# Block 1 works on rows that are not yet normed: the norm applied when results leave PSUM, and the modulation sums tied to their place

## The chip, the cores and the metric

The kernel is one program on one core of a Trainium2 chip. The metric is the device time of one execution in microseconds (us): the median of several runs, lower is better.

## What is computed

Two blocks follow each other on 256 tokens of width 1024, all in float32. Block 1 has two layers, and the change lies in them:

```python
def hybrid_layer(x, gain, w_in, f_bias, w_branch, w_out):
    h = rms_norm(x, gain)                       # x * rsqrt(mean(x*x) + eps) * gain
    proj = jnp.einsum('bsd,de->bse', h, w_in)
    (qa, ka, va, ga, qb, kb_, vb_, gb, qc, kc, vc, gc,
     q_idx, k_idx, w_idx, f_logit, merge_logit) = jnp.split(proj, SPLIT_POINTS, axis=-1)
    ...
    # branch a: attention with rotary positions; branch b: the same over the keys that an
    # index (q_idx, k_idx, w_idx) selects; branch c: attention with forgetting (f_logit)
    y = jnp.einsum('nbsw,nwd->bsnd', jnp.stack([oa, ob, oc], axis=0), w_branch)
    merged = jnp.sum(jax.nn.sigmoid(merge_logit).reshape(B, S, N_BRANCH, D_MODEL) * y, axis=2)
    return x + jnp.einsum('bsd,de->bse', merged, w_out)
```

The second block (a Fourier and gating mixer, a neighbourhood attention, two gated feed-forward nets) is modulated by six vectors of each layer, `silu(c) @ ada_w + ada_b`, for two conditions.

The norm's factor is one number per token. So `rms_norm(x, gain) @ W` equals `(x * gain) @ W` with each token's row scaled afterwards.

## The kernel before, in words

Every product of activations and weights is done three times, with both split in a rounded high part and a remainder (`hh`, `hl` for activations, `whi`, `wlo` for weights): high by high, high by low, low by high. TensorE (PE) takes 128 tokens or 128 features at a time.

Weights come in pieces of 512 KB (`piece`, L159 to L173): SP issues the load into one of three `raw` buffers, ScalarE (ACT) writes `whi` (L171), VectorE (DVE) writes `wlo` (L172), and with that the raw buffer is free for the next load. A chunk is four pieces, 1024 by 512 weights. SP is one queue, and a load that waits for its buffer holds back what is behind it.

**The head of layer 0 (L813 to L844).** PE is kept busy by ten products on a tile of zeros (`keep_up`, L252 to L254). For each of the two rows of 128 tokens: ACT squares two halves of x and adds them up (L294), a root and a few DVE steps make the factor (`rstd`, L305 to L320), DVE scales the row (`xs`, L325), PE turns it in eight transposes of 128x128 (L341), ACT and DVE evacuate them with the gain (`hf`, L351 and L347), ACT writes `hh` (L356), DVE writes `hl` (L358). The weight splits are held behind the norm on their engines (`behind`). Then `layer(0, ...)` begins.

**A layer (L444 to L811)** runs: the first chunk (index queries, `heads_T` with kind "first": row 0's 24 products, then row 1's), the small projections (`psm`: index keys, index weights, forget logits), the four chunks of branch a (q, k, v, gate), the selection for branch b, branch b's chunks between the parts of branch a's attention, branch c's, three merges, and `w_out` in two column halves, whose second half gives row 0, then row 1. As soon as a row is finished, `done0` squares, norms, turns and splits it for layer 1.

**The modulation sums (`ada`, L372 to L426)** are done on DVE: for each 512 KB tile of `ada_w` and each condition one multiply-add over 1024 columns (L417 the first of a group, L419 the rest); after eight tiles PE adds up the partitions (`reduce`, L384 to L396, product L388 `pada`), and the result goes to memory. A generator yields one tile at a time; `fill` (L179) advances it two steps at every second call, from the end of branch a's attention on. That is the place in the program. The tool that lays out the queues orders each engine's instructions by when it thinks that they can start, and among those by place in the program, so these sums may be issued much earlier than they are written.

The index scores of the selection go through `psc`'s two PSUM buffers too (tag "at"); ACT evacuates them (`r`, L662), and DVE weighs them (L667).

Of the kernel before, what the change touches and what calls it, by code (L numbers as in the profile page):

```python
# [92 lines left out]
def tile_model(ctx: ExitStack, tc: tile.TileContext, A: dict, out: bass.AP, dbg=None):  # L93
# [170 lines left out]

    def mm_feat(ps, pieces, m, xh, xl):
        mm_group(pieces, [feat_target(ps, m, xh, xl)])
# [14 lines left out]
    class Row:  # L281
# [51 lines left out]
        def norm_steps(self, gains, shifts, hh, hl, o, last, xs=None, even=False):  # L333
            if xs is None:
                xs = self.scaled()
            for g in range(2):
# [35 lines left out]
    def ada(tasks):  # L372
# [28 lines left out]
        for i, (layer, g, k) in enumerate(tiles):  # L401
# [24 lines left out]
    def block1(pa):  # L426
# [17 lines left out]
        def layer(l, hT, done, first):  # L444
            W = A["w_in"][l]
            hh, hl = hT

            def tok(t):
                return slice(t * P, (t + 1) * P)

            def heads_T(pieces, kind, scale, dst):

                pss = [ps_mm(nm("pq")) for t in range(2)]
                tg = [tok_target(pss[t], hh, hl, tok(t)) for t in range(2)]
# [25 lines left out]
            def values(pieces):  # L480
                v = pt.tile([P, 2, 512], F32, tag="v", bufs=2, name=nm("v"))
                pss = [ps_mm(nm("pv")) for t in range(2)]
                mm_group(pieces, [tok_target(pss[t], hh, hl, tok(t)) for t in range(2)])
                for t in range(2):
                    ACT.activation(v[:, t, :], pss[t], AF.Copy)
# [93 lines left out]
            mm_feat(ps[:, :S], sw, 0, hh, hl)  # L579
# [6 lines left out]
            DVE.tensor_copy(sm, ps[:, :S])  # L586
# [96 lines left out]
            def project(b):  # L683
# [5 lines left out]
                def heads(i, scale, dst):  # L689
                    if b < 2:  # L690
                        heads_T(chunk(W[4 * b + i]), "rope", scale, dst)
# [3 lines left out]
                def v_():  # L695
                    r["v"] = values(chunk(W[4 * b + 2]))
# [91 lines left out]
            for c2 in range(2):  # L788
# [30 lines left out]
        w0 = pa.tile([P, 1], F32, name="w0")  # L819
        ACT.activation(w0, one, AF.Sqrt)  # L820
# [649 lines left out]
```

## Time and profile before

| | us |
|---|---|
| median of 3 runs | 1599.95 |
| lowest, highest | 1597.28, 1603.94 |
| the profiled execution | 1600.51 |
| its span, first to last instruction | 1598.7 |
| PE busy | 1574.8 (99%) |
| VectorE (DVE) busy | 1187.3 (74%) |
| ScalarE (ACT) busy | 796.4 (50%) |

An engine's busy time is the union of its instructions. PE's instructions are recorded with a modelled end: products of 512 columns are shown with 0.40 us each while they start every 0.23 us, so PE's throughput is read from starts. PEclk is the clock that PE was granted, as a share of 2.4 GHz; 0.5 is 1.2 GHz.

### The profile page before, as it was taken

To read this page: it belongs to the slowest core of one execution; us is meant where nothing else is said; L and a number is where in the kernel's file an instruction comes from. 1 tells how busy PE (TensorE), PEld (TensorE's weight loads), DVE (VectorE), ACT (ScalarE), POOL (GpSimd) and SP (SyncE) were. 2 spreads that over 40 slices of the span, in tenths; PEclk is the share of its full clock that TensorE was granted. 3 is DMA by queue.
4 is the path that set the end of the run, shared out by engine and by line. 5 is a ranking of instruction groups with operands and counts; after the bars stand their busy time and mean duration, and the time that the engine had idled before them with its cause. 6 is when DMAs were issued, how large, how long until landed. Compare 5 with 4: busy or idle time off the path is not lost.

```text
span 1598.7 us, 24860 instructions
## 1 busy us (share of the span) xinstructions
PE 1574.8 (99%) x9397; PEld 1325.4 (83%) x9397; DVE 1187.3 (74%) x2262; ACT 796.4 (50%) x1351; POOL 29.0 (2%) x45
## 2 busy tenths in 40 slices
PE   9999999999999999999999999999999999999999
PEld 7868898978888999878898877877787677679897
DVE  7996557877877779888678599776668656588773
ACT  6555545555555455664354332333345545576551
POOL 0000000000000000000000000000000201000000
PEclk9999999999999999999999999999999999999999
DMA  7753555746445757544335356755535323367650
GB/s 259 243 174 120 158 184 171 226 143 202 150 142 190 222 175 236 171 169 136 96 117 183 106 196 221 248 190 176 180 104 147 97 68 113 91 220 242 210 181 27
DMA packets 81496, 267.21 MB, mean 167 GB/s; under 512 B 10400, under 2 KB 16736, under 8 KB 81376
## 3 DMA queue, kind: packets, MB, share of 16 engines
q1 hardware_dynamic: 81376, 265.62, 52.3%
q8 instruction: 74, 1.21, 0.3%
q14 instruction: 46, 0.38, 0.1%
HBM read 264.45 MB, written 1.13 MB: 166 GB/s over the span
## 4 chain that ended last, share of the span: by engine, by line
PE 86%; DVE 6%; ACT 3%; DMA 3%; issue 2%; SPq 0%; DVEq 0%; ACTq 0%
PE pfg L239 4%; PE pfg L241 4%; PE pfd L1201 4%; PE pfv L241 4%; PE pfv L239 4%; PE pfv L240 4%; PE pfg L240 4%; PE pfd L1203 4%; PE pfd L1202 4%; PE pmg L239 3%; PE pmg L241 3%; PE pmg L240 2%; DVE wlo L172 2%; PE pq L231 2%; PE psc L515 2%
## 5 line engine op out<-in xcount | busy, mean ns | idle before, releaser
L171 ACT ACTIVATE whi<-raw 128x1024 fp32r<-128x1024 f32 x390 | 407.3, 1050 | 396.7 <-PE pfd L1203 51.7
L172 DVE TENSOR_TENSOR wlo<-raw,whi 128x1024 fp32r<-128x1024 f32 x390 | 470.0, 1211 | 156.8 <-ACT whi L171 154.7
L419 DVE SCALAR_TENSOR_TENSOR adaa<-adaw,cs,adaa 128x1024 f32<-128x1024 f32 x140 | 176.8, 1279 | 11.9 <-DMA adaw<-in_ada_w 11.4
L241 PE MATMUL pfg<-hh,wlo 128*128 128x256 f32 (+1 forms) x352 | 117.7, 334 | 0.0
L239 PE MATMUL pfg<-hh,whi 128*128 128x256 f32 (+1 forms) x352 | 117.5, 334 | 0.1
L239 PE MATMUL pfv<-hh,whi 128*128 128x256 f32 (+1 forms) x352 | 117.3, 333 | 0.1
L241 PE MATMUL pfv<-hh,wlo 128*128 128x256 f32 (+1 forms) x352 | 117.3, 333 | 0.0
L240 PE MATMUL pfv<-hl,whi 128*128 128x256 f32 (+1 forms) x352 | 116.9, 332 | 0.0
L240 PE MATMUL pfg<-hl,whi 128*128 128x256 f32 (+1 forms) x352 | 116.7, 331 | 0.0
L239 PE MATMUL pmg<-hh,whi 128*128 128x256 f32 x384 | 108.2, 282 | 0.0
L241 PE MATMUL pmg<-hh,wlo 128*128 128x256 f32 x384 | 107.7, 280 | 0.0
L240 PE MATMUL pmg<-hl,whi 128*128 128x256 f32 x384 | 107.3, 279 | 0.0
L1201 PE MATMUL pfd<-whi,gh 128*128 128x512 f32 (+1 forms) x275 | 105.7, 386 | 0.0
L1203 PE MATMUL pfd<-whi,gl 128*128 128x512 f32 (+1 forms) x275 | 105.7, 384 | 0.0
L1202 PE MATMUL pfd<-wlo,gh 128*128 128x512 f32 (+1 forms) x275 | 105.5, 384 | 0.0
L239 PEld LDWEIGHTS pfg<-hh,whi 128*128 128x128 f32 x352 | 66.2, 188 | 8.5 <-issue 1.5
L239 PEld LDWEIGHTS pmg<-hh,whi 128*128 128x128 f32 x384 | 72.2, 188 | 1.2 <-issue 0.8
L240 PEld LDWEIGHTS pfv<-hl,whi 128*128 128x128 f32 x352 | 66.3, 188 | 7.5
L240 PEld LDWEIGHTS pfg<-hl,whi 128*128 128x128 f32 x352 | 66.3, 188 | 7.5
L239 PEld LDWEIGHTS pfv<-hh,whi 128*128 128x128 f32 x352 | 66.1, 188 | 7.5 <-issue 0.5
L240 PEld LDWEIGHTS pmg<-hl,whi 128*128 128x128 f32 x384 | 72.2, 188 | 0.2 <-issue 0.2
L241 PEld LDWEIGHTS pmg<-hh,wlo 128*128 128x128 f32 x384 | 72.2, 188 | 0.0
(338 smaller groups left out, 3801.6 us busy)
## 6 DMA issues: line engine op xcount, KB each, us to landing
raw<-in_w_in SPq DMA_DIRECT2D x152, 512.0 KB
adaw<-in_ada_w SPq DMA_DIRECT2D x96, 512.0 KB
raw<-in_ffn_up SPq DMA_DIRECT2D x96, 512.0 KB
raw<-in_ffn_down SPq DMA_DIRECT2D x40, 512.0 KB
raw<-in_w_branch SPq DMA_DIRECT2D x24, 512.0 KB
raw<-in_odd_qkv SPq DMA_DIRECT2D x24, 512.0 KB
raw<-in_w_out SPq DMA_DIRECT2D x16, 512.0 KB
raw<-in_even_in SPq DMA_DIRECT2D x12, 512.0 KB
```

The costliest lines, as they stand in the source:

```text
L171: behind(ACT.activation(hi, raw, AF.Copy))
L172: behind(DVE.tensor_sub(lo, raw, hi.bitcast(F32)))
L231: PE.matmul(ps, xl[:, k, tsl], hi, start=False, stop=last)
L239: PE.matmul(ps, hi[:, msl], xh[:, k, :], start=first, stop=False)
L240: PE.matmul(ps, hi[:, msl], xl[:, k, :], start=False, stop=False)
L241: PE.matmul(ps, lo[:, msl], xh[:, k, :], start=False, stop=last)
L419: behind(DVE.scalar_tensor_tensor(acc[:, s, :], raw, c, acc[:, s, :], op0=ALU.mult, op1=ALU.add))
L515: PE.matmul(pss[j][:, o_:o_ + n], qT[64 * j:64 * j + 64, hp, qs_], kT[64 * j:64 * j + 64, hp, ks_], start=terms is None, stop=True)
L1201: PE.matmul(ps, gh[:, k, tsl], hi[:, i, csl], start=k == 0, stop=False)
L1202: PE.matmul(ps, gh[:, k, tsl], lo[:, i, csl], start=False, stop=False)
L1203: PE.matmul(ps, gl[:, k, tsl], hi[:, i, csl], start=False, stop=k == NH - 1)
```

## The change

In both layers, the first chunk, the small projections and branch a's q, k and v are computed from `x * gain` (tiles `raw`), without the norm's factor. The factor is worked out meanwhile (`roots`) and multiplied in where ACT or DVE takes the result out of PSUM. After branch a's k, `normalize` makes the normed `hh` and `hl` for all later chunks: two small products spread the factors of the tokens over the partitions, and DVE and ACT scale and split the turned rows again. In layer 0 the three products of a piece run as high by high, low by high, high by low, row 0 then row 1, piece by piece (`mm_parts`). At the boundary of the layers the rows are turned column half by column half as the halves of `w_out` finish, each of them queued for the end of a group of products (`later`). In the head, the identity is loaded ahead of x, row 1 of x after the first piece of weights, and ten filler products become four and eight (the eight on x). The modulation sums are pinned: none is issued ahead of the DVE instruction that is written just before it. The activations with a root, at the head and at the boundary, go away in block 1's layer 0.

```diff
+    SP.dma_start(cst[:, 0:P], A["cst"][:, 0:P])
     for n in range(2):
         SP.dma_start(x_sb[:, 0, n * 512:n * 512 + 512], A["x"][0:P, n * 512:n * 512 + 512])
-    SP.dma_start(cst[:, 0:P], A["cst"][:, 0:P])
     SP.dma_start(vec, A["vec"])
-    SP.dma_start(x_sb[:, 1, :], A["x"][P:2 * P, :])
...
+    def pinned(ins):
+        behind(ins)
+        tc.keep_in_program_order(ins)
...
+    def mm_parts(rows_, pieces, xh, xl):
+        n, k0 = len(pieces), 0
+        for j, (hi, lo, nk) in enumerate(pieces):
+            for ps, tsl in rows_:
+                for part, (x_, w_) in enumerate(((xh, hi), (xl, hi), (xh, lo))):
+                    for i in range(nk):
+                        p_ = PE.matmul(ps, x_[:, k0 + i, tsl], w_[:, i, :], start=j == part == i == 0,
+                                       stop=j == n - 1 and part == 2 and i == nk - 1)
+                        if part == i == 0:
+                            tc.keep_in_program_order(p_)
+            k0 += nk
...
-                    behind(DVE.tensor_scalar_mul(acc[:, s, :], raw, c))
+                    pinned(DVE.tensor_scalar_mul(acc[:, s, :], raw, c))
...
-                    behind(DVE.scalar_tensor_tensor(acc[:, s, :], raw, c, acc[:, s, :], op0=ALU.mult, op1=ALU.add))
+                    pinned(DVE.scalar_tensor_tensor(acc[:, s, :], raw, c, acc[:, s, :], op0=ALU.mult, op1=ALU.add))
...
+            def normalize():
+                ps = ps_tr(nm("prb"))
+                for t in range(2):
+                    b_ = sp.tile([P, P], F32, tag="t512", bufs=4, name=nm("rb"))
+                    DVE.tensor_scalar_mul(b_, C("ones"), rs[0][:, t:t + 1])
+                    PE.matmul(ps[:, tok(t)], b_, ident, start=True, stop=True)
+                rb = pt.tile([P, S], F32, tag="t256", bufs=3, name=nm("rb"))
+                DVE.tensor_copy(rb, ps[:, :S])
+                for g in range(2):
+                    ks = slice(4 * g, 4 * g + 4)
+                    f = sp.tile([P, 4, S], F32, tag="big", bufs=2, name=nm("hn"))
+                    tc.keep_in_program_order(DVE.tensor_add(f, rh[:, ks, :].bitcast(F32), rl[:, ks, :].bitcast(F32)))
+                    DVE.tensor_mul(f, f, rb.unsqueeze(1).broadcast_to([P, 4, S]))
+                    split_to(hh[:, ks, :], hl[:, ks, :], f)
...
                 if kind == "first":
-                    for t in range(2):
-                        mm_group(pieces, [tg[t]])
-                else:
-                    mm_group(pieces, tg)
+                    rs.append(root())
+                    rs.append(sp.tile([P, 2], F32, tag="rs8", bufs=1, name=nm("rs8")))
+                    DVE.tensor_scalar_mul(rs[1], rs[0], 0.125)
...
-                    ACT.activation(qs, ps, AF.Copy, scale=scale)
+                    ACT.activation(qs, ps, AF.Copy, scale=scale if kind == "rope" else r_[:, t:t + 1])
...
+                if f is steps[1]:
+                    normalize()
...
-                        xr[t].square(a, w)
+                        if l == 1:
+                            xr[t].square(a, w)
...
                     load_ahead(*first)
+                    if l == 0:
+                        later(turn_first)
...
+        def roots():
+            ss = sp.tile([P, 2, 2], F32, tag="rss", bufs=8, name=nm("rss"))
+            for t in range(2):
+                for n in range(2):
+                    junk = sp.tile([P, 512], BF16, tag="jx", bufs=1, name=nm("junk"))
+                    behind(ACT.activation(junk, x_sb[:, t, n * 512:n * 512 + 512], AF.Square, accum_out=ss[:, t, n:n + 1]))
+            v = sp.tile([P, 2], F32, tag="rsv", bufs=8, name=nm("rsv"))
+            DVE.tensor_add(v, ss[:, :, 0], ss[:, :, 1])
+            DVE.tensor_scalar(v, v, 1.0 / D, EPS, op0=ALU.mult, op1=ALU.add)
+            return rsqrt(v, 2)
+
+        def turn_first():
+            raw_tiles()
+            for t in range(2):
+                turn(t, 0)
...
         with tc.high_priority():
-            keep_up(ps, 10, idle)
+            keep_up(ps, 4, idle)
+        turn(0, 0, True)
+        load_ahead("qi0", A["w_in"][0][12], 1)
+        SP.dma_start(x_sb[:, 1, :], A["x"][P:2 * P, :])
+        keep_up(ps, 8, x_sb[:, 0, :])
+        turn(0, 1)
+        turn(1, 0, True)
+        load_ahead("qi0", A["w_in"][0][12], 2)
+        turn(1, 1, True)
         load_ahead("qi0", A["w_in"][0][12])
...
         def done0(t):
-            if t == 0:
-                nxt.append(h_tiles())
-            xr[t].norm_T(V("ng1"), None, nxt[0][0], nxt[0][1], t * P, True)
-            if t == 0:
-                load_ahead("qi1", A["w_in"][1][12])
+            def rest():
+                turn(t, 1, True)
+                if t == 0:
+                    load_ahead("qi1", A["w_in"][1][12])
+            later(rest)
```

`turn(t, g)` transposes four 128-column blocks of row t (half g of the columns) and writes `raw`'s high and low part with the gain, by the steps that `norm_steps` had. `rsqrt` (L269 to L280) is eleven small DVE steps.

## Rows read from the trace of the kernel before

**Rows 1.** The page's first part: busy us (share of the span) xinstructions.

```profile
PE 1574.8 (99%) x9397; PEld 1325.4 (83%) x9397; DVE 1187.3 (74%) x2262; ACT 796.4 (50%) x1351; POOL 29.0 (2%) x45
```

**Rows 2.** Table of stretches: length, busy PE, PEld, DVE, ACT, POOL; PEclk, DMA, GB/s.

```profile
26.00:60.00 34.00, 33.12 (x181) 26.60 (x180) 30.88 (x68) 18.32 (x24) 0.00 (x0) 1.00 0.80 263
...
82.00:98.00 16.00, 12.96 (x46) 9.45 (x45) 13.75 (x40) 7.82 (x17) 0.00 (x0) 0.79 0.46 143
...
110.00:240.00 130.00, 129.71 (x975) 115.99 (x973) 79.98 (x170) 69.89 (x127) 0.00 (x0) 1.00 0.51 159
340.00:362.00 22.00, 20.23 (x93) 15.51 (x92) 17.69 (x31) 13.69 (x28) 1.25 (x4) 0.92 0.37 120
362.00:440.00 78.00, 77.43 (x431) 63.73 (x430) 63.33 (x180) 44.68 (x68) 0.00 (x0) 1.00 0.56 172
```

**Rows 3.** The same table over the first part of each of the two layers.

```profile
20.00:110.00 90.00, 86.07 (x459) 69.82 (x458) 81.03 (x197) 50.32 (x78) 0.00 (x0) 0.96 0.68 219
340.00:440.00 100.00, 97.66 (x521) 79.24 (x520) 81.02 (x210) 58.37 (x95) 1.25 (x4) 0.98 0.52 161
```

**Rows 4.** The table of stretches, for the tile `adaa` alone: PE, PEld and DVE.

```profile
20.00:110.00 90.00, 0.00 (x0) 0.00 (x0) 19.29 (x16) 0.96 0.68 219
```

**Rows 5.** Timeline of the head, PE: start, us, instruction [idle before <-releaser].

```profile
1.48 6.87 PE L254 MATMUL pidle<-idle 128*128 128x256 f32 x20 [1.48 <-DVE idle L823]
...
8.63 1.89 PE L254 MATMUL pidle<-xs 128*128 128x256 f32 x8
...
11.40 0.49 PE L229 MATMUL pq<-whi,hh 128*128 128x512 f32 x1 [0.44 <-ACT hh L356]
...
25.29 0.40 PE L230 MATMUL pq<-wlo,hh 128*128 128x512 f32 x1
25.52 0.39 PE L231 MATMUL pq<-whi,hl 128*128 128x512 f32 x1
```

**Rows 6.** Timeline of the head, ACT and DVE.

```profile
3.51 0.63 ACT L294 ACTIVATE junk<-x_sb 128x512 bf16<-128x512 f32 x1 [1.28 <-DMA x_sb<-in_x]
...
8.93 0.86 ACT L351 ACTIVATE hf<-pT,vec 128x128 f32<-128x128 f32 x3
...
9.82 0.35 DVE L347 TENSOR_SCALAR hf<-pT,vec 128x128 f32<-128x128 f32 x1 [0.42 <-ACT hf L351]
...
10.73 0.61 ACT L356 ACTIVATE hh<-hf 128x512 fp32r<-128x512 f32 x1
```

**Rows 7.** Timeline of PE, then of ACT, where layer 0's branch a begins to attend.

```profile
88.12 2.13 PE L515 MATMUL psc<-qk 64*128 64x128 f32 x8 [2.48 <-ACT r L662]
...
86.53 1.06 ACT L171 ACTIVATE whi<-raw 128x1024 fp32r<-128x1024 f32 x1 [2.49 <-DMA raw<-in_w_in]
87.49 1.07 ACT L662 ACTIVATE r<-pix 128x512 f32<-128x512 f32 x2
```

**Rows 8.** What SP's queue waited for, 0 to 110 us: total, times, longest.

```profile
SPq L168 <- DVE wlo L172: 38.1, 14, 8.0
```

**Rows 9.** Timeline of PE at the boundary of the layers.

```profile
352.09 0.66 PE L469 MATMUL pqT<-cst,qs 128*128 128x128 f32 x4 [1.12 <-DVE hf L347]
...
354.13 0.66 PE L231 MATMUL pq<-whi,hl 128*128 128x512 f32 x1 [0.55 <-DVE hl L358]
```

**Rows 10.** Groups by line, 0 to 60 us: count | busy us, mean ns | idle before.

```profile
L606 PE MATMUL pcum<-lf,cst 128*128 128x8 f32 x2 | 0.4, 256 | 0.0
...
L172 DVE TENSOR_TENSOR wlo<-raw,whi 128x1024 fp32r<-128x1024 f32 x18 | 21.8, 1222 | 3.8 <-ACT whi L171 3.7
...
L586 DVE COPY sm<-psm 128x256 f32<-128x256 f32 x1 | 0.4, 418 | 0.0
...
L319 DVE SCALAR_TENSOR_TENSOR rsy<-rst,rsy 128x1 f32<-128x1 f32 x2 | 0.3, 159 | 0.1
```

**Rows 11.** The tile `adaa` over the span: durations min/median/max ns; idle time ahead (us, times).

```profile
L419 DVE SCALAR_TENSOR_TENSOR adaa<-adaw,cs,adaa x140: 1252/1280/1292, 31.2 to 1167.5; 128x1024 f32<-128x1024 f32 x140
...
  DMA adaw<-in_ada_w: 11.4, 10
```

More of the change, by code (lines that the diff above doesn't have):

```diff
@@ L331, in norm_T, with norm_steps @@
                 pass
-        def norm_steps(self, gains, shifts, hh, hl, o, last, xs=None, even=False):
+        def norm_steps(self, gains, shifts, hh, hl, o, last, xs=None, even=False, halves=(0, 1)):
             if xs is None:
                 xs = self.scaled()
-            for g in range(2):
+            for g in halves:
                 ps = ps_tr(nm("pT"))
@@ L442, in rope, with layer @@
             DVE.tensor_add(q3[:, :, 0:16], q3[:, :, 0:16], tmp)
-        def layer(l, hT, done, first):
+        def layer(l, raw, hT, root, done, first):
             W = A["w_in"][l]
             hh, hl = hT
+            rh, rl = raw
+            rs = []
             def tok(t):
                 return slice(t * P, (t + 1) * P)
+            def normalize():
[12 more added lines that the diff above has]
+                    split_to(hh[:, ks, :], hl[:, ks, :], f)
@@ L451, in heads_T @@
             def heads_T(pieces, kind, scale, dst):
                 pss = [ps_mm(nm("pq")) for t in range(2)]
-                tg = [tok_target(pss[t], hh, hl, tok(t)) for t in range(2)]
-                if kind == "first":
-                    for t in range(2):
-                        mm_group(pieces, [tg[t]])
-                else:
-                    mm_group(pieces, tg)
+                xh, xl = (hh, hl) if kind == "rope" else raw
+                if kind == "first" and l == 0:
+                    mm_parts([(pss[t], tok(t)) for t in range(2)], pieces, xh, xl)
+                elif kind == "first":
+                    for t in range(2):
+                        mm_group(pieces, [tok_target(pss[t], xh, xl, tok(t))])
+                else:
+                    mm_group(pieces, [tok_target(pss[t], xh, xl, tok(t)) for t in range(2)])
@@ L478, in plain_T, with values @@
                 fill()
-            def values(pieces):
+            def values(pieces, b):
                 v = pt.tile([P, 2, 512], F32, tag="v", bufs=2, name=nm("v"))
                 pss = [ps_mm(nm("pv")) for t in range(2)]
-                mm_group(pieces, [tok_target(pss[t], hh, hl, tok(t)) for t in range(2)])
+                mm_group(pieces, [tok_target(pss[t], *((hh, hl) if b else raw), tok(t)) for t in range(2)])
                 for t in range(2):
-                    ACT.activation(v[:, t, :], pss[t], AF.Copy)
+                    ACT.activation(v[:, t, :], pss[t], AF.Copy, scale=1.0 if b else rs[0][:, t:t + 1])
                 fill()
@@ L690, in heads @@
                     if b < 2:
-                        heads_T(chunk(W[4 * b + i]), "rope", scale, dst)
+                        heads_T(chunk(W[4 * b + i]), "rope" if b else "raw", scale, dst)
                     else:
@@ L818, in block1, with raw_tiles, turn @@
         hT = h_tiles()
-        w0 = pa.tile([P, 1], F32, name="w0")
-        ACT.activation(w0, one, AF.Sqrt)
+        raw = []
+        def raw_tiles():
+            raw[:] = [pa.tile([P, KD, S], F32R, tag=g, bufs=n, name=nm("raw" + g)) for g, n in (("mac", 1), ("qk", 3))]
+        raw_tiles()
+        def turn(t, g, last=False):
+            for _ in xr[t].norm_steps(V(turn.gain), None, *raw, t * P, last, xr[t].ap, halves=(g,)):
+                pass
+        def roots():
+            ss = sp.tile([P, 2, 2], F32, tag="rss", bufs=8, name=nm("rss"))
+            for t in range(2):
+                for n in range(2):
[6 more added lines that the diff above has]
+        def turn_first():
+            raw_tiles()
+            for t in range(2):
+                turn(t, 0)
+        turn.gain = "ng0"
         idle = sp.tile([P, 512], F32, tag="t512", bufs=4, name="idle")
@@ L825, in block1 @@
         with tc.high_priority():
-            keep_up(ps, 10, idle)
+            keep_up(ps, 4, idle)
[7 more added lines that the diff above has]
+        turn(1, 1, True)
         load_ahead("qi0", A["w_in"][0][12])
         SP.dma_start(cst[:, P:], A["cst"][:, P:_C1])
-        with tc.high_priority():
-            for t in range(2):
-                for n in range(2):
-                    xr[t].square(n * 512)
-                xs = xr[t].scaled()
-                steps = xr[t].norm_steps(V("ng0"), None, hT[0], hT[1], t * P, t == 1, xs)
-                if t == 0:
-                    for _ in range(5):
-                        next(steps)
-                    keep_up(ps, 4, xs)
-                for _ in steps:
-                    pass
         for l in range(2):
@@ L862, in done1 @@
                 xr[t].square(n * 512)
-        layer(0, hT, done0, ("qi1", A["w_in"][1][12], 2))
+        turn.gain = "ng1"
+        layer(0, raw, hT, roots, done0, ("qi1", A["w_in"][1][12], 2))
         filler[0] = None
@@ L867, in block1 @@
         SP.dma_start(fg, A["final_gain"][0:1, :].broadcast_to([P, D]))
-        layer(1, nxt[0], done1, ("ev", A["even_in"][2], 2))
+        layer(1, raw, hT, roots, done1, ("ev", A["even_in"][2], 2))
     xr = [Row(x_sb[:, t, :]) for t in range(2)]
```

10 lines of the change are left out of this document (5 added, 5 removed).

## The prediction

> **What bounds the kernel now.** I read the page first: PE is busy for 99% of the span, DVE for 74% [rows 1]. So the time can only fall where PE idles, runs at its lower clock or does work that the result doesn't need, and such places have to be looked for one by one. The table of stretches shows three in block 1's layer 0 and at the boundary to layer 1. In 82 to 98 us PE is busy 12.96 of 16.00 us, 3.04 short, and its mean granted clock is 0.79; since the clock has two levels, 2.4 and 1.2 GHz, 0.21 of 16 us, 3.36 us, is lost on top: 6.40 us. In 340 to 362 us it is 1.77 us of idling and 0.08 x 22 = 1.76 us of clock: 3.53 us. In 26 to 60 us it is 0.88 us [rows 2]. Elsewhere in these parts it is little: 0.57 us in 362 to 440, 0.29 us in 110 to 240 [rows 2]. The fourth place is the head: the first real product starts at 11.40 us, the last of the first chunk at 25.52 us [rows 5].
>
> Then the timeline, for the causes. In the head the first 14 us go into reading x, squares, the factor, the scaled row, transposes and splits, one behind the other [rows 6]. At 85 to 88 us PE waits 2.48 us for ACT's `r`; ACT itself had sat 2.49 us for a piece of weights, with `r` queued behind that split [rows 7]. The piece was late because SP waits for raw buffers: 38.1 us in 14 waits for DVE's `wlo` up to 110 us [rows 8]. So the engine behind the stall is DVE: busy 81.03 of 90 us there, of which 19.29 us are modulation sums, issued long before their place in the program [rows 3, 4]. At the boundary PE waits for the turned row 1, 1.12 and 0.55 us, and then runs at 1.2 GHz for a while [rows 2, 9].
>
> **The change, part by part.** Sums are made against the profiled execution, 1600.51 us (span 1598.7 and 1.8 around it); it lies 0.56 us above the median of the runs shown.
>
> *Head.* The squares, the factor and the scaled row go from the path; the transposes wait for x alone, whose first half is there at 3.51 us, and for PE, which first does eight filler instructions instead of twenty. Twenty took 6.87 us from 1.48 on, so eight end at about 1.48 + 8/20 x 6.87 = 4.2 us. The first four transposes end near 4.8. Then stand sixteen filler instructions on x (each product is recorded as two), at 1.89/8 = 0.24 us [rows 5]: to 8.6 us. The other transposes, and with them the first product, which is pinned behind the last of them, wait for that and for PSUM: its two transpose buffers are freed by ACT's 0.86 and DVE's 0.35 us [rows 6], so the last four run near 10.5 to 11 us. The first product starts at about 11.4 us, as now. What is won is the stretch behind it: 48 products at 25.52 - 25.29 = 0.23 us are 11.2 us, and they took 25.52 + 0.23 - 11.40 = 14.35 us because row 1's norm was in between [rows 5]. ACT has four times 0.86 + 0.61 for the rows [rows 6] and four splits of 1.06 [rows 7], 10.1 us between 4.8 and 18: they keep up. I take 0.5 us for waits: end at 23.1, **2.7 us won**. The bounds: with the filler fitted into waits the first product starts at 8.6, the end is 11.2 and some 1.5 us of transposes later, 21.3: 4.4 won. At the other end, PE at its lower clock at the start: in 82 to 98 us a drop cost 3.36 us [rows 2], which would leave 0.7 us lost. I take full clock, because x is there at 3.51 us, before the filler ends, so that PE has work without a break from 1.48 us on. The Trainium skill (TensorE: Matmul & The Clock Gate, What's actually happening) says that PE's default state is the throttled one and that activity releases it, which speaks against cutting the filler; by it the head would be at the lower bound if PE paused between filler and transposes, and no row of before shows such a pause.
>
> The squares (four of 0.63 on ACT [rows 6]) and the factor (some 14 DVE steps of 0.16 [rows 10], 2.2 us) now lie beside PE's first chunk and small projections; if that cover is gone, the evacuation of the first chunk comes up to 2 us late. SP's queue is moved too: row 1 of x goes behind the first piece of weights, which is so ahead of it by 512 KB; no cost, since row 1 is wanted after the filler.
>
> *Pinned sums.* The first sum can't be issued before branch c's second chunk, past 110 us. So 19.29 us leave DVE's 81.03 [rows 3, 4], and SP's loads of `ada_w` no longer stand in between. Layer 1 is the comparison: the same code in 362 to 440 us, with hardly any sums and DVE at 63.33 of 78, loses 0.57 us [rows 2]. I take **5.8 of the 6.40 us** in 82 to 98, and **0.4 of the 0.88** in 26 to 60; bounds 0 and all of both. At their new place, 110 to 240 us, DVE has 79.98 + 19.29 of 130 [rows 2, 4], 76%, which covers them: nothing. If that cover is gone, see the first rival.
>
> *Boundary.* Half of each row is turned while `w_out` still runs, the second half of row 0 behind row 1's products, that of row 1 between the two rows of the first chunk; behind it stand 12 products on the half that is ready, 2.8 us, against 0.86 + 0.35 + 0.61 us of evacuation [rows 6] and a remainder. The factor isn't wanted there. **3.5 us won**; bounds 1 and 3.53, the lower if DVE is 2.5 us late.
>
> *Normalising.* For each layer PE gets two float32 products with their four instructions, priced as an upper bound by 0.256 us each [rows 10], 1.0 a layer; taken 0.75 each, **1.5 us lost** (bounds 0.4 and 2). DVE gets two adds, two multiplications and two subtractions over 1024 columns, at 1.22 us like `wlo`, a copy of 0.42 [rows 10] and two small steps: 8.3 us. In layer 0, 19.29 us less make room: 81.0 - 19.3 + 8.3 + 2.2 = 72.2 us. In layer 1 nothing does but the old norm's few: 81.02 becomes about 88 of 100 us, the load that layer 0 has now, 90% [rows 3]. There a loss stands between nothing and layer 0's 0.88 + 6.40 = 7.3 us [rows 2]; I take **1.5**, nearer to nothing, because layer 0's stall had SP's extra loads with it and layer 1 won't.
>
> Sum: -2.7 - 5.8 - 0.4 - 3.5 + 1.5 + 1.5 = **-9.4 us**, 1591.1 of the profiled execution, 1590.5 by the median. All best ends together give -14.8 (4.4 + 6.40 + 0.88 + 3.53 - 0.4), 1585.
>
> **Rivals.** *The partitions' sum waits for its last products (slower).* `reduce` is written straight behind the last tile's two multiply-adds, which are now pinned there, where before they were done early. PE is then held by DVE's queue, up to two sums of 1.28 us [rows 11], twelve times (six vectors, two layers): 12 x 2.56 = 31 us, so 1621. From a mean wait of (9.4 + 8)/12 = 1.45 us on the result is slower by over 8 us. For it: a sum that waits for its weights did hold DVE, 11.4 us in ten waits [rows 11]. Against: PE has other chunks that may be issued ahead of `reduce`, and the tool knows the order. The Trainium skill (TensorE: Matmul & The Clock Gate, the table ahead of What a matmul computes) states that VectorE's queue is strictly first in, first out; by this rule a pinned sum that waits for its load stops the splits behind it too, and the trace agrees with the 11.4 us named. 9%.
>
> *The stall moves to layer 1 (no change).* The head's and the boundary's 6.2 us come, layer 0's 6.2 too, but normalising costs layer 1 the whole 7.3: -12.4 + 1.5 + 7.3 = -3.6, 1596.3. For it: DVE at 88%, and branch a's gate waits for `normalize`. 27%.
>
> *The change doesn't do what it says (no change).* The late weights at 86 us are SP's and HBM's matter, not the sums', and the filler keeps the head as it was: -3.5 + 1.5 + 1.5 = -0.5, 1599.4. For it: DMA at 0.80 of its time in 26 to 60 us [rows 2]. 8%.
>
> **How the numbers follow.** The forecast, 1590.5, has 56%, mostly at 1585 to 1594. A measurement of this kernel tells about 0.5%, 8 us, from no change, so 1592 is the line to faster. Of the forecast's 56, 52 lie below it; of the second rival's 27, 4: faster 0.56. Slower has 8 of the first rival's 9. The rest, 0.36, is no change. The range takes in the best ends with the 0.57 us of layer 1 besides, and above it the second and the third rival: 1584 to 1600.
>
> **What would show it.** In the new trace: the last product of the first chunk near 23 us; no sum before 110 us; PE full and at clock 1.0 in what was 82 to 98; at the boundary no wait for `hf` or `hl`. Wrong would be: PE waiting before `pada`; a stall at `pg` or `psc` in layer 1 behind `normalize`; or a clock below 1 in the first 12 us.

## The result, and the profile after

The change makes the kernel slower: 1615.09 us median (1614.52 to 1616.80, 4 runs) beside 1600.16 for the kernel before on the same chip (1597.28 to 1603.94), a ratio of 1.0094 with the interval 1.0071 to 1.0116. The profiled execution took 1614.52 us, its span is 1612.7. In the page's first part, which answers to [rows 1], PE is busy 5.3 us more while the span is 14.0 us longer: most of the loss is PE standing still.

```profile
PE 1580.1 (98%) x9401; PEld 1326.4 (82%) x9401; DVE 1208.0 (75%) x2282; ACT 798.3 (49%) x1343; POOL 29.2 (2%) x45
```

The table of stretches over the windows of [rows 2] (length, busy PE, PEld, DVE, ACT, POOL; PEclk, DMA, GB/s):

```profile
26.00:60.00 34.00, 32.69 (x179) 26.25 (x178) 26.85 (x73) 20.16 (x28) 0.00 (x0) 1.00 0.72 222
82.00:98.00 16.00, 15.24 (x73) 11.41 (x72) 15.68 (x42) 11.06 (x21) 0.00 (x0) 1.00 0.55 172
110.00:240.00 130.00, 129.95 (x991) 116.86 (x990) 87.55 (x168) 68.12 (x126) 0.00 (x0) 1.00 0.55 174
340.00:362.00 22.00, 20.97 (x106) 17.03 (x104) 13.69 (x29) 12.93 (x25) 0.98 (x4) 1.00 0.53 163
362.00:440.00 78.00, 76.04 (x410) 62.21 (x411) 70.03 (x192) 45.67 (x69) 0.00 (x0) 0.98 0.52 158
```

In 82 to 98 us PE is busy 15.24 us at clock 1.00, where it was 12.96 at 0.79: the stall is gone, and 110 to 240 us stays full with the sums in it. The loss must lie outside these windows. To find it, I took the start of the same PE instruction in both traces (the k-th one into a tile of the same name) and subtracted. A row of this table is one such instruction; the first number is its start before, the others are the differences of the kernels that the experiments below explain (us):

| instruction | before | after | e8 | e12 | e2 | e5 | e1 | e3 | e9 | e7 | e10 | e4 | e11 |
|---|---|---|---|---|---|---|---|---|---|---|---|---|---|
| first `psm` (end of layer 0's first chunk) | 25.7 | 0.0 | +0.1 | -2.1 | +0.5 | -2.0 | -1.4 | -1.6 | -1.8 | +0.7 | +0.3 | +1.1 | +0.5 |
| first `po` (layer 0, branch a) | 117.7 | -4.6 | -3.0 | -3.7 | -6.6 | -5.4 | -3.7 | -4.6 | -4.6 | -6.3 | -6.7 | -5.7 | -5.3 |
| `pix` of layer 1 | 390.3 | -0.5 | -0.1 | -1.0 | -4.2 | -2.1 | -4.9 | -3.9 | -4.7 | -5.4 | -6.6 | -4.7 | -2.2 |
| a `pmg` of layer 1 | 568.6 | +0.2 | +0.1 | -0.8 | -4.2 | -1.1 | -4.2 | -2.7 | -4.6 | -4.4 | -6.5 | -4.7 | -0.9 |
| first `pfg` (feed-forward) | 817.8 | +12.4 | +15.6 | +4.7 | +11.8 | +8.5 | -2.7 | -0.4 | -2.9 | -3.3 | -5.7 | -3.3 | -1.3 |
| near the end | 1594.3 | +14.0 | +16.3 | +5.9 | +13.1 | +11.3 | +1.2 | +1.8 | -2.4 | -0.7 | -5.4 | -3.7 | -1.6 |

So the changed kernel has a gain of 4.6 us at 118 us, has given it back by 390, and loses 12.2 us between 569 and 818, in a part whose instructions the diff changes in no other way than by the pins (it also moves tiles in SBUF, of which more below). The table of stretches between these two products, of the kernel before and of the changed one:

```profile
568.60:817.80 249.20, 246.27 (x1521) 210.41 (x1520) 200.58 (x404) 133.38 (x256) 0.00 (x0) 1.00 0.47 151
568.80:830.10 261.30, 250.53 (x1520) 211.45 (x1519) 210.10 (x410) 135.86 (x256) 0.00 (x0) 0.99 0.48 151
```

PE idles 2.93 us in the first and 10.77 in the second: 7.8 of the 12.2 us are waits. What PE waited for in 640 to 820 us of the changed kernel (total, times, longest):

```profile
PE pfa L1136 <- DVE al L382: 2.9, 1, 2.9
PE pab L1123 <- ACT ah L381: 2.3, 1, 2.3
PE pw L234 <- DVE wlo L176: 2.2, 1, 2.2
PE pT L358 <- DVE xs L342: 1.3, 1, 1.3
PE pT L358 <- DVE hf L366: 1.3, 1, 1.3
```

The timeline of DVE ahead of the first and third of these, and PE's two instructions that end the waits:

```profile
657.67 4.87 DVE L436 SCALAR_TENSOR_TENSOR adaa<-adaw,cs,adaa 128x1024 f32<-128x1024 f32 x4
662.45 1.22 DVE L176 TENSOR_TENSOR wlo<-raw,whi 128x1024 fp32r<-128x1024 f32 x1
...
663.73 0.50 PE L234 MATMUL pw<-wlo,mh 128*128 128x512 f32 x1 [2.23 <-DVE wlo L176]
...
779.58 4.87 DVE L436 SCALAR_TENSOR_TENSOR adaa<-adaw,cs,adaa 128x1024 f32<-128x1024 f32 x4 [0.66 <-DMA adaw<-in_ada_w]
...
784.98 0.42 DVE L382 TENSOR_TENSOR al<-pfa,ah 128x256 fp32r<-128x256 f32 x1
...
785.45 0.39 PE L1136 MATMUL pfa<-dfh,abh 128*128 128x256 f32 x1 [2.89 <-DVE al L382]
```

Here four pinned sums stand in one block of 4.87 us, and the split that PE needs stands right behind, or one instruction later. The second wait, `pab`, and the two of `pT`, at 693.64 and 695.99 us, are of another kind. DVE's last sums ahead of them, the next sums, and PE's instruction that ends the wait of `pab`:

```profile
673.65 2.47 DVE L436 SCALAR_TENSOR_TENSOR adaa<-adaw,cs,adaa 128x1024 f32<-128x1024 f32 x2
...
750.40 1.41 DVE L434 TENSOR_SCALAR adaa<-adaw,cs 128x1024 f32<-128x1024 f32 x2
...
716.91 0.39 PE L1123 MATMUL pab<-dfh,ah 128*128 128x256 f32 x1 [2.35 <-ACT ah L381]
```

No sum stands on DVE between 676.1 and 750.4 us. What is new is PE's order: `pab` needs the evacuation of products `pef` and now stands right behind the first 24 of the 96; before the change it stands behind all 96 and waits for nothing.

After the wait at 663.73 PE runs at the lower of its two clocks for a while: 664 to 668 us has a mean granted clock of 0.57, where the kernel before has 1.00; 0.43 of 4 us is another 1.7 us lost.

Two smaller places are new. The timeline of the head, PE and then ACT:

```profile
5.06 0.91 PE L358 MATMUL pT<-cst,x_sb 128*128 128x128 f32 x4
...
12.46 1.10 PE L358 MATMUL pT<-cst,x_sb 128*128 128x128 f32 x4 [2.16 <-DVE hf L364]
13.21 1.20 PE L276 MATMUL pq<-whi,rawmac 128*128 128x512 f32 x2
...
6.71 1.28 ACT L368 ACT_TABLE_LOAD   x1 [6.71 <-DMA vec<-in_vec]
8.00 0.88 ACT L368 ACTIVATE hf<-pT,vec 128x128 f32<-128x128 f32 x3
```

ACT's first instruction is now the first evacuation, so the load of its function table, 1.28 us, stands on the path behind the gains' arrival at 6.71. PE waits 2.16 us for an evacuated transpose buffer, its first product starts at 13.21 us where it started at 11.40 [rows 5], and its first six products run at the lower clock (0.66 on the mean of 12 to 17 us). The 48 products then run without a break, and the small projections start where they did.

At the boundary the transposes' waits [rows 9] are gone, and this wait stands a few microseconds further on (PE, then ACT, then DVE):

```profile
363.30 0.50 PE L233 MATMUL pq<-whi,rawmac 128*128 128x512 f32 x1 [2.33 <-ACT qs L508]
...
361.62 1.06 ACT L175 ACTIVATE whi<-raw 128x1024 fp32r<-128x1024 f32 x1 [1.83 <-DMA raw<-in_w_in]
362.58 1.25 ACT L508 ACTIVATE qs<-pq,rsy 128x512 f32<-128x512 f32 x2
...
359.55 1.22 DVE L176 TENSOR_TENSOR wlo<-raw,whi 128x1024 fp32r<-128x1024 f32 x1 [0.92 <-ACT whi L175]
360.69 0.15 DVE L295 SCALAR_TENSOR_TENSOR rsy<-rst,rsy 128x2 f32<-128x2 f32 x1
```

The last step of the factor ends at 360.84 us. The evacuation `qs`, which takes the factor in, starts at 362.58 only, because on ACT it stands behind a split that waits 1.83 us for its weights.

### The profile page after: what moved, and what is told of

Its sections match the earlier page's. It is cut to its first block, busy times and chain, and to the rows that moved or that the text cites. A ratio compares the mean times of both kernels' runs of the same rounds, so it can differ in the third digit from the quotient of the medians.

```text
span 1612.7 us, 24879 instructions
## 1 busy us (share of the span) xinstructions
PE 1580.1 (98%) x9401; PEld 1326.4 (82%) x9401; DVE 1208.0 (75%) x2282; ACT 798.3 (49%) x1343; POOL 29.2 (2%) x45
## 4 chain that ended last, share of the span: by engine, by line
PE 78%; DVE 10%; DMA 6%; ACT 4%; issue 2%; SPq 0%; DVEq 0%; ACTq 0%
PE pfd L1276 4%; PE pfd L1277 4%; PE pfd L1278 4%; PE pfv L243 4%; PE pfg L245 4%; PE pfv L244 4%; PE pfv L245 4%; PE pfg L243 4%; PE pfg L244 4%; DVE wlo L176 4%; PE pmg L243 2%; PE pmg L245 2%; PE pmg L244 2%; ACT whi L175 2%; DMA raw<-in_w_in 1%
## 5 line engine op out<-in xcount | busy, mean ns | idle before, releaser
L436 DVE SCALAR_TENSOR_TENSOR adaa<-adaw,cs,adaa 128x1024 f32<-128x1024 f32 x140 | 172.9, 1280 | 8.7 <-DMA adaw<-in_ada_w 8.5
L245 PEld LDWEIGHTS pfv<-hh,wlo 128*128 128x128 f32 x352 | 66.3, 188 | 7.0
```

Of the source, the lines that this page charges most:

```text
L245: PE.matmul(ps, lo[:, msl], xh[:, k, :], start=False, stop=last)
L436: pinned(DVE.scalar_tensor_tensor(acc[:, s, :], raw, c, acc[:, s, :], op0=ALU.mult, op1=ALU.add))
```

## The experiments

Ratios are to the kernel before, run on the same chip; a difference of two ratios is turned into us with 1600.

**Which half: pins or norm.** One kernel takes the pins off the change, one adds them alone (both for the multiply-add too).

```diff
 e1_unpinned (changed kernel)
-  pinned(DVE.tensor_scalar_mul(acc[:, s, :], raw, c))
+  behind(DVE.tensor_scalar_mul(acc[:, s, :], raw, c))
...
 e2_pins_alone (kernel before)
-  behind(DVE.tensor_scalar_mul(acc[:, s, :], raw, c))
+  pinned(DVE.tensor_scalar_mul(acc[:, s, :], raw, c))
...
```

> The changed kernel without the pins. Theory P (the pins are what costs: from 326 us on blocks of pinned sums, up to 4.87 us on DVE, stand ahead of splits and evacuations that PE waits for, some 14 us by 830 us, while they win some 5 us at 82 to 98): the stall in layer 0 comes back, the waits at 661, 714 and 782 us go; 1603 to 1608 us. Theory N (the moved norm costs: its extra vector work and shifted order cause the later waits too): the later waits stay and the layer 0 stall comes on top, 1617 to 1621 us.

> The kernel before with all sums pinned and nothing else. Theory P: about -5 us in layer 0 and +12 to +14 from 326 us on, so 1606 to 1611 us, with the waits at w_out of layer 1 and in the mixer. Theory N: the pins are a gain without the norm, 1593 to 1596 us.

Measured: e1 1602.13 us (ratio 1.0007, 0.9997 to 1.0018), e2 1612.64 (1.0064, 1.0049 to 1.0079). The pins alone bring 10.2 us of loss, and without them 1.1 us are left (e2 is 1.6 us above theory P's range, e1 0.9 us below it). PE's waits of 580 to 820 us in e1 (total, times, longest):

```profile
PE pef L243 <- DVE vn L1090: 1.7, 1, 1.7
PE psg L1147 <- DVE sg L1149: 0.9, 1, 0.9
PE pT L358 <- DVE hf L366: 0.6, 1, 0.6
```

The amount of work is the same in both: the table of stretches for `adaa` alone has 16 sums in 700 to 820 us of the changed kernel, after 18 in 580 to 700:

```profile
700.00:820.00 120.00, 18.50 (x16) 1.00 0.37 115
```

The same table of e1 has 14, after 18 too:

```profile
700.00:820.00 120.00, 17.81 (x14) 1.00 0.34 106
```

What differs is where they stand. In DVE's timeline of e1 the 14 are issued one by one but for the last two, all between 702 and 747 us, where the changed kernel has none; the first two:

```profile
702.19 1.28 DVE L436 SCALAR_TENSOR_TENSOR adaa<-adaw,cs,adaa 128x1024 f32<-128x1024 f32 x1
708.71 1.28 DVE L436 SCALAR_TENSOR_TENSOR adaa<-adaw,cs,adaa 128x1024 f32<-128x1024 f32 x1
```

PE's order differs with them. In the ten kernels whose groups (0,3) and (0,4) aren't pinned (the kernel before, e1, e3, e4, e6, e7, e9 to e12), the first `pab` stands behind all 96 products `pef` and PE doesn't wait for it; in the four where they are (the changed kernel, e2, e5, e8), it stands behind 24 and PE waits 2.35 to 3.04 us. How the pins lead the tool to this order, the runs don't show.

**Only the first group pinned.** The stall at 82 to 98 us concerned the sixteen sums of group (0,0) alone [rows 4].

```diff
-  behind(...)      (e3: pinned(...))
+  (pinned if (layer, g) == (0, 0) else behind)(...)
   e3_first_group: in the changed kernel; e4_first_group_alone: in the kernel before
```

> The changed kernel with only the first group's 16 sums pinned (those that stood in 20 to 110 us); all later groups free as before. Theory P: layer 0's win stays, the later cost goes; block 1 ends level with before or 2 us ahead, 1597 to 1601 us. Theory N: the later waits stay, 1612 to 1616 us.

> The kernel before with only the first group's 16 sums pinned. Theory P, and the reading of the stall at 82 to 98 us as made by these sums: the stall (3.04 us of idling and 3.36 of clock) goes and nothing else changes, 1594 to 1596 us. If the late weights there are SP's and the memory's matter: 1599 to 1601 us.

Measured: e3 1603.57 us (1.0014, 1.0003 to 1.0025), 2.6 us above what was expected of it; e4 1596.60 (0.9970, 0.9959 to 0.9982), faster than both kernels and 0.6 us above its range. The table of stretches of e4 (columns as above):

```profile
82.00:98.00 16.00, 15.43 (x73) 11.32 (x72) 14.81 (x40) 10.38 (x21) 0.00 (x0) 1.00 0.55 176
```

So the pin's own purpose holds: it earns 5.7 us at 118 us in the table above and about 4 at the end. But e3, with the same pin, doesn't keep it, although none of the late waits is left. Something else in the change costs.

**One step at a time.** If blocks of four are the harm, blocks of two might do.

```diff
         owed[0] = owed[0] + n if filler[0] is not None else 0
-        if owed[0] < 2:
+        if owed[0] < 1:
```

> The changed kernel with all its pins; only `fill` differs: it advances the modulation one tile (two sums, 2.4 us of DVE) at every call instead of two tiles (four sums, 4.87 us) at every second call. The same sums, the same pins, the same stretch. Theory G (grouping): the loss of 12 to 13 us against the unpinned version comes from four sums standing in one block ahead of a split or an evacuation that PE waits for; with 2.4 us less in front of them the four long waits of 2.2 to 2.9 us and the 1.7 us each that the half clock costs behind them mostly go: 1603 to 1608 us, and the waits at pw, pab and pfa at 650 to 790 us are under 0.6 us each. Theory L (load): these stretches have no room on DVE for the sums, however they are cut: 1612 to 1617 us, with as much waiting in more, shorter waits.

Measured: 1613.18 us (1.0080, 1.0063 to 1.0097), as theory L said, but the run doesn't separate the two. Its edit reaches only calls that ask for one step; the mixer calls `fill(4)`, and in DVE's timeline the blocks there stayed:

```profile
769.49 4.87 DVE L436 SCALAR_TENSOR_TENSOR adaa<-adaw,cs,adaa 128x1024 f32<-128x1024 f32 x4
775.48 5.06 DVE L436 SCALAR_TENSOR_TENSOR adaa<-adaw,cs,adaa 128x1024 f32<-128x1024 f32 x4
```

Where it did reach, the wait at `pw` at 663 us went, and a longer one came at `pT` (2.9 us in two). So it stays open whether four sums in one block do more harm than the same sums in twos. The question was put again in e12, below.

**Two parts of the norm half.** e6 gives ACT its table before the gains arrive; e7 keeps head and layer 0 of the kernel before and takes the change at the boundary and in layer 1. Both pin group (0,0) alone.

```diff
 e6_table_early (e3)
+        w0 = pa.tile([P, 1], F32, name="w0")
+        ACT.activation(w0, one, AF.Copy)
         ada_pool[0] = pa
         hT = h_tiles()
 e7_layer1_only (e3)
-        turn(0, 0, True)
...
+                    xr[t].square(n * 512)
+                xs = xr[t].scaled()
+                steps = xr[t].norm_steps(V("ng0"), None, hT[0], hT[1], t * P, t == 1, xs)
...
+                if l == 0 and kind != "first":
+                    kind = "rope"
...
-        layer(0, raw, hT, roots, done0, ("qi1", A["w_in"][1][12], 2))
+        layer(0, hT, hT, None, done0, ("qi1", A["w_in"][1][12], 2))
```

> The version with only group (0,0) pinned (e3_first_group, 1603.6 us) plus one ACT copy of a constant as ACT's first instruction, so that the table load of 1.28 us that stood on the path behind the load of the gains at 6.7 us is done before. Theory T (the table was on the path): the first evacuation starts at 6.7 to 6.9 us in place of 8.0, the small projections start 1.0 to 1.3 us before 24.2 us, and 1602.0 to 1602.8 us. Theory W (weights and row 1 of x bind): the first evacuation is earlier, but the small projections start at 24.0 to 24.4 us, and the time is 1603 to 1604.5 us. In both the gain of the head may be lost again between 27 and 42 us, where the version without the table edit lost 3.5 us against the kernel before.

> The kernel before with group (0,0) pinned (e4_first_group_alone, 1596.6 us) plus the change at the boundary and in layer 1 alone: head, first chunk and layer 0 as in the kernel before, layer 1's first chunk, small projections and branch a from rows not normed. Theory P (the prediction's term for the boundary holds): the transposes' waits go, nothing replaces them: 3.5 us less, 1592 to 1594 us. Theory D (the head of layer 1 is given back): the first chunk ends some 4.5 us earlier, and 3 us of it are lost by 390 us in waits behind the factor, the splits of the normed rows and the loads: 1595 to 1597.5 us.

Measured: e6 1609.14 us (1.0049, 1.0035 to 1.0063), e7 1601.55 (1.0006, 0.9997 to 1.0016). Both are far above all that was expected. For the head e6 does answer: the first evacuation starts at 6.36 us in place of 8.02 in e3, yet the small projections start at 24.17 us in both. That is as theory W has it: row 1 of x, now loaded behind a piece of weights, and its two evacuations are what the head ends on; PE waits 0.43 us for `x_sb` in e6 and 0.87 in e3. But the filler on x also ends 1.5 us later in e6, and the run doesn't tell the two apart.

By the medians e6 lost 5.6 us to e3, in the profiled executions 6.7. Of these, 2.7 are there by 60 us and have a wait behind them:

```profile
43.46 0.36 PE L650 MATMUL pcum<-lf,cst 128*128 128x8 f32 x2 [2.21 <-issue]
```

After it PE runs at the lower clock for a while (0.63 on the mean of 44 to 48 us). Another 4.5 us have no wait behind them; they grow evenly from 114 to 570 us. I therefore read the pitch of undisturbed products, the time from the start of one to the start of the next. PE's timeline has 96 products `pmg` in a row; the first and the last of them in e3:

```profile
217.33 0.28 PE L243 MATMUL pmg<-hh,whi 128*128 128x256 f32 x1
...
228.52 0.28 PE L245 MATMUL pmg<-hh,wlo 128*128 128x256 f32 x1
```

The same two in e9, a later kernel that computes the same:

```profile
216.95 0.28 PE L243 MATMUL pmg<-hh,whi 128*128 128x256 f32 x1
...
228.03 0.28 PE L245 MATMUL pmg<-hh,wlo 128*128 128x256 f32 x1
```

And in e11:

```profile
217.23 0.28 PE L244 MATMUL pmg<-hh,whi 128*128 128x256 f32 x1
...
228.63 0.28 PE L246 MATMUL pmg<-hh,wlo 128*128 128x256 f32 x1
```

The 95 steps take 11.19, 11.08 and 11.40 us, that is 117.8, 116.6 and 120.0 ns each; in the kernel before 11.09, in the changed one 11.19, in e6 11.40. The kernels with one pitch have one thing in common: where `hh` starts in SBUF. In the built programs it starts, counted modulo 128 bytes, at 64 (before, e2, e4), at 96 (changed kernel, e1, e3, e5, e7) and at 0 (e6). The change's new tile `rs8` takes 32 bytes in front of it, and e6's `w0` another 32. The same holds for `pfd` in block 2, whose `gh` starts at 96 before and at 0 after. The first and the last of 137 such products in a row, in PE's timeline of e3:

```profile
959.07 0.50 PE L1277 MATMUL pfd<-wlo,gh 128*128 128x512 f32 x1
...
990.91 0.40 PE L1278 MATMUL pfd<-whi,gl 128*128 128x512 f32 x1
```

And of e9:

```profile
956.02 0.50 PE L1279 MATMUL pfd<-wlo,gh 128*128 128x512 f32 x1
...
987.27 0.40 PE L1280 MATMUL pfd<-whi,gl 128*128 128x512 f32 x1
```

The 136 steps take 31.84 and 31.25 us, 234.1 and 229.8 ns each; the kernel has 825 products `pfd`, 759 of them of 512 columns.

**The same kernels with the tiles where they were.** `rs8` moves among tiles that exist, `w0` comes back behind `hl`; in e11 the tiles of the kernel e4 are moved on purpose, to where the weights start.

```diff
 e8_after_placed (changed kernel), e9_first_group_placed (e3), e10_layer1_only_placed (e7)
-  rs.append(sp.tile([P, 2], F32, tag="rs8", bufs=1, name=nm("rs8")))
+  rs.append(sp.tile([P, 2], F32, tag="rsr", bufs=8, name=nm("rs8")))
   (e8, e9)
         hT = h_tiles()
+        w0 = pa.tile([P, 1], F32, name="w0")
+        DVE.memset(w0, 0.0)
 e11_at_32 (e4)
+        w0 = pa.tile([P, 1], F32, name="w0")
         hT = h_tiles()
-        w0 = pa.tile([P, 1], F32, name="w0")
...
+        DVE.memset(sp.tile([P, 16], F32, tag="gap", bufs=1, name="gap"), 0.0)
```

> The changed kernel, nothing computed otherwise; only two small tiles are laid out as in the kernel before (the new tile `rs8` takes a place among the tiles `rsr`, and the tile `w0` stands behind `hl` again), so that `hh`, `hl` and every later tile of block 1 and of block 2's pools start at the same addresses as before and not 32 bytes higher. Theory A (address): the pitch of the products follows the start addresses: 256 columns on `hh` from 117.8 back to 116.7 ns (some 2200 products), the 825 products `pfd` from 233.3 back to 229.5 ns; 2.4 + 3.1 us less: 1609 to 1610.5 us. Theory N (not the address): the pitches stay and the time with them, 1613 to 1616.5 us.

> e3_first_group (the whole change with only group (0,0) pinned, 1603.6 us) with the same two tiles laid out as in the kernel before. Theory A: 5.5 to 6 us less, 1597 to 1599 us, which makes the norm part of the change worth nothing or a loss of up to 2 us against e4_first_group_alone (1596.6 us, the same pins and addresses without the norm part). The prediction's terms for head, boundary, `normalize` and congestion (together 3.6 us less, with the prices of the two `normalize` taken off) would give 1593 us. Theory N: 1602.5 to 1605 us.

> e7_layer1_only (head and layer 0 of the kernel before, boundary and layer 1 of the change, group (0,0) pinned, 1601.6 us) with the tiles of block 1 and block 2 at the addresses of the kernel before. There the products `py` on `oh`, `ol` ran at 119.9 ns for 117.8 and `pfd` at 233.3 for 229.5, `pmg` and `pg` at 117.8 for 116.7. Theory A: 3.1 us for `pfd`, 2.4 us for the products on `hh`, 1.2 us for `py`: 1594.5 to 1596 us, that is the boundary's part worth 1 to 2 us against e4_first_group_alone (1596.6 us). Theory N: 1600.5 to 1602.5 us.

> e4_first_group_alone (the kernel before with group (0,0) pinned, 1596.6 us) with 64 bytes more in front of the pools and `w0` ahead of `hh`: the activations `hh`, `hl`, `oh`, `ol`, `mh`, `ml` of block 1 and `gh`, `gl` of block 2 then start 32 bytes above a multiple of 128, as the weights do. Over nine kernels the products of 512 columns had 228.4 to 229.4 ns in the one place where both operands start so (pow), and 233.3 ns with the activations at 64 or 96. Theory A: 4 to 5 ns off each of some 1340 products of 512 columns in block 1, 6 us, and for the 2900 of 256 columns, which no kernel has had there, something between 113 and 118 ns in place of 116.7 to 117.8: 0 to 10 us: 1580 to 1591 us. Theory N: 1595 to 1598 us.

Measured: e8 1614.97 us (1.0093, 1.0078 to 1.0108), e9 1598.48 (0.9997, 0.9988 to 1.0006), e10 1595.61 (0.9974, 0.9965 to 0.9982), e11 1599.56 (0.9998, 0.9989 to 1.0008). In all four the pitch followed the address: in e8 to e10 `pmg` runs at 116.7 ns again and `pfd` at about 230. The time followed in e9 (2.7 us less than e3 by the ratios) and e10 (5.1 less than e7). In e8 it did not: its time is what theory N said, although the pitch changed. Its profiled execution, the slowest of its four, has waits as long as the changed kernel's or longer (`pfa` 2.9 us, `pab` 2.7, `pw` 2.4) and runs at the lower clock behind two more of them (0.83 in 715 to 725 and in 785 to 795 us, where the changed kernel's has 1.00). That faster products only wait longer for DVE would fit, but isn't shown. e11 was a miss: at 32 the products of 512 columns in block 1 gained about 1 ns and `pfd` 2 ns, but those of 256 columns went to 119 to 120 ns, so the kernel is 4.5 us slower than e4 by the ratios.

**Two groups free.**

```diff
 e12_two_groups_free (e8)
-  pinned(...)
+  (behind if (layer, g) in ((0, 3), (0, 4)) else pinned)(...)
```

> e8_after_placed (the whole change with all pins, tiles at the addresses of the kernel before, 1615.0 us) with the pin taken from two groups of modulation sums alone, (0,3) and (0,4): 32 of the 160 sums, whose place is between 596 and 792 us of the changed kernel; the other 128 stay pinned, (0,5) and the six of layer 1 in the feed-forward among them. Theory Q (a few places): the loss comes from where these two groups stand, in blocks ahead of the splits of w_out, of the mixer's first chunks and of its Fourier part; the four waits of 2.2 to 2.9 us at pw, pT, pab and pfa go with their half clock: 1598 to 1602 us, beside 1598.5 us with only (0,0) pinned. Theory R (every pinned group costs its share, for DVE has no room anywhere): 32 of 144 sums are freed, 3 to 4 us of the 16.5 us that the pins of groups after (0,0) cost: 1610 to 1613 us.

Measured: 1604.78 us (1.0021, 1.0011 to 1.0030), between the two, nearer to Q: 32 of the 144 sums pinned behind group (0,0) carry 0.0072 of their 0.0096, that is 11.5 of 15.4 us. PE's waits of 580 to 820 us in e12:

```profile
PE pT L358 <- DVE xs L342: 3.7, 4, 1.7
PE pef L243 <- DVE vn L1092: 1.8, 1, 1.8
PE pada L405 <- DVE adaa L436: 0.7, 1, 0.7
```

`pfa`, `pab` and `pw` are gone. Beside e9 the ratios leave 3.8 us, the two profiled executions 8.3 (e12's was its slowest run, e9's its median); the table has it in pieces, 0.9 us by 118 us, 3.7 by 390 (the blocks ahead of `mh` and the boundary), 7.6 by 818 (the `xs` of the rows after layer 1 among it). Which of the remaining pins causes each was not tried.

## Why the prediction was wrong

The prediction gave 1590.5 us and 0.08 to slower. The step that failed is the price of nothing for the pinned sums at their new place; the head and the boundary, also forecast as gains, brought none. The parts add up, in ratios of kernels whose tiles lie alike:

| part | from | to | us | predicted |
|---|---|---|---|---|
| group (0,0) pinned | before | e4, 0.9970 | -4.8 | -6.2 |
| the other 144 sums pinned | e4 and e9, 0.9970 and 0.9997 | e2 and e8, 1.0064 and 1.0093 | +15.0 and +15.4 | 0 |
| boundary and layer 1 | e4, 0.9970 | e10, 0.9974 | +0.6 | -1.3 |
| head and layer 0's norm | e10, 0.9974 | e9, 0.9997 | +3.7 | -2.0 |
| together | | | +14.7 | -9.4 |

(-3.5 + 0.75 + 1.5 = -1.25 for the boundary with layer 1's normalising, -2.7 + 0.75 = -1.95 for the head; the +14.7 takes 15.2 for the second part; measured in all: +15.0.) For the head and for the boundary the intervals reach about 2 us to either side, so the boundary's part can't be told from none.

**Pinned sums at their old stall: right.** The first sum stands at 157 us, PE is full in 82 to 98, and SP's loads no longer come between (no load of `ada_w` is issued between 16.2 and 158.1 us). The term was 5.8 and 0.4; 5.7 us are there at 118 us in e4. In e1, without any pin, there is no drop of the clock either at 82 to 98: six of the sixteen sums had moved behind 110 us with the rest of the change. So the pin is one way, not the only one, to undo that stall.

**Pinned sums at their new place: the step that failed.** "At their new place, 110 to 240 us, DVE has 79.98 + 19.29 of 130, 76%, which covers them: nothing." The working looked at the sixteen sums that leave layer 0's start and found room for them; there it holds. It didn't ask what the pin does to the other 144. The tool had issued them mostly one by one, and PE idled 2.93 us from 569 to 818 us. Pinned, many come in blocks of 4.87 us where `fill` is called, and what counts there is not DVE's share over 100 us but what stands behind the block: `wlo` and `al`, for which PE waits 2.23 and 2.89 us. And the pins changed PE's own order, with waits of 2.35 us at `pab` and 2.5 at `pT` behind no sum. DVE's share says nothing on either; it is 78% in 700 to 820 us in both kernels. That the pins cause the loss is shown by e1, e2, e4 and e12; what of it is blocks and what is order, no run separates.

**First rival: the side was right, the mechanism wrong.** PE hardly waits before `pada` (0.7 us in two waits of the changed kernel). The sentence that goes with it, on VectorE's queue being strictly first in, first out (the Trainium skill, TensorE: Matmul & The Clock Gate, the table ahead of What a matmul computes), is what the traces show, with splits as those who wait: 2.23 us at 663.73 and 2.89 at 785.45. I had drawn it only for a sum that waits for its load; here it is mostly sums that were ready (of the block at 779.58 us, 0.66 us are such a wait). Its price, 1621 us, came near by chance, and its 9% was far too little.

**Head: -2.7 predicted, nothing measured in the changed kernel, a gain of 1.4 to 2.1 us in six others, and a loss behind it.** The working gave ACT's first evacuation the price of an evacuation; the table load of 1.28 us that the removed root had done early was missed, and so were the gains, which land at 6.71. (The working also has 48 products at 0.23 us as 11.2 us; they are 11.0, which changes nothing here.) The executions with the old head in e2, e4, e7, e10 and e11 have their first `psm` 0.3 to 1.1 us later than the kernel before, so beside those the gain is nearer to the 2.7. "Full clock" was wrong too: after the wait of 2.16 us the first products run at the lower level, and the sentence that the Trainium skill (TensorE: Matmul & The Clock Gate, What's actually happening) has on the throttled default agrees with that. It isn't so after every pause: e3, with a wait of 1.76 us at that place, shows no drop (1.00 in 12 to 17 us). "No cost" for row 1 of x doesn't hold in e3 and e6, where PE waits 0.87 and 0.43 us for it; the changed kernel shows no such wait. And what the head gains is lost in the next stretch. PE's waits in 26 to 57 us of e9:

```profile
PE pqT L514 <- ACT smT L626: 1.4, 1, 1.4
PE pcum L650 <- PE pq L235: 0.6, 1, 0.6
PE pki L683 <- DVE dup L682: 0.5, 1, 0.5
```

And of e10, which has the old head:

```profile
PE pki L686 <- DVE rope L458: 0.3, 1, 0.3
```

That is 2.5 us against 0.3: behind the first chunk PE now waits mostly for evacuations. In 26 to 60 us of the changed kernel PE idles 1.31 us for 0.88 [rows 2], so the 0.4 us hoped for there didn't come either.

**Boundary: 3.5 predicted, 1.9 left at 390 us.** e10 against e4 in the table: -6.6 and -4.7. The waits of [rows 9] and the drop of the clock do go. "The factor isn't wanted there" holds for the transposes; it is wanted by `qs`, and the prediction named that price in the head ("if that cover is gone, the evacuation of the first chunk comes up to 2 us late") without carrying it to the boundary. In the changed kernel it is 2.33 us of waiting and a mean clock of 0.57 in 364 to 368 us, but 1.7 of the 2.33 are the split ahead of `qs` on ACT: the factor was there at 360.84. In e1, e3, e5, e7 to e10 and e12, which have the new boundary too, this wait is 0.3 to 1.1 us.

**Normalising in layer 1: nothing to speak of.** 362 to 440 us lose 1.96 us of PE in the changed kernel for 0.57 before [rows 2], and the last 1.3 of the 2.33 us above explain the difference. The second rival had no case.

## What to carry to other kernels

Before an instruction is tied to its place in the program, look at every place that it will stand in, ask what stands right behind it on that engine and how soon it is wanted, and look at whether the order of the other engines' instructions changed with it; a share of busy time over a stretch doesn't answer this. Tie only the instances that do harm: the sixteen sums of the first group are worth 5 us, and the other 144 cost 15. When a kernel with more or fewer small tiles is compared with another, compare the pitch of untouched products as well: e10, 1595.61 us, and e4, 1596.60, are the best versions found, both faster than the two kernels compared here and not to be told from each other, and the first of them, as e7, looked like a loss beside e4 until 32 bytes were given back.

## What was not expected of the hardware

- The pitch of products depends on where their operands start in SBUF; e8 to e11 change nothing else but for a memset. With weights that start at 32 (modulo 128 bytes), products of 256 columns on activations that start at 64, 96, 0 and 32 take 116.7, 117.8, 120.0 and 119 to 120 ns each. For `pfd`, where the 512 columns are those of the weights and the activations are the stationary operand, `gh` at 96, 0 and 32 gives 229.8, 234.1 and 227.8 ns over 137 in a row. Why, the runs don't show; only these offsets were tried.
- The table load is recorded as 1.28 us and the next activation follows at once (6.71 + 1.28 = 7.99, start 8.00).
- A wait of 2.2 to 2.3 us was followed by a stretch at the lower clock at 12, 364 and 664 us of the changed kernel, but not every wait of that length was: behind the 2.89 us at 785 us the mean granted clock stays at 1.00 there (784 to 794 us), while e8, with the same 2.9 us, has 0.83 in 785 to 795.
